# Hybrid sub-block of a two-layer net: SSD tiles of two head pairs, dt's exponentials behind the last silu, outputs split four chunks at a time

## The chip, the cores and the metric

One core of a Trainium2 chip runs the whole program. The metric is device microseconds (us) of one execution. Engines: TensorE (PE, with its weight loader PEld) multiplies, VectorE (DVE) and ScalarE (ACT) do elementwise work, GpSimd (POOL) a few masks, and SyncE (SP) issues the DMAs. Each engine runs its instructions strictly in the order in which the program lists them.

## The reference, cut to what matters

256 tokens of width 1024 pass through six sub-blocks (FFN, hybrid, FFN; FFN, mLSTM, FFN), each with a modulated RMS norm before it and a gated residual after it, all in float32. The change lies in the hybrid:

```
gate_lru, x_lru, z_ssd, xbc, dt_raw = split(h @ w_in)
y_lru = rg_lru(conv(x_lru)) * gelu(gate_lru)          # a_t, u_t = gates; h_t = a_t h_{t-1} + u_t, u has a sqrt
xbc   = silu(conv(xbc));  xs, B, C = split(xbc)       # 16 heads of 64, 2 groups, state 128
dt    = softplus(dt_raw + bias);  a = -exp(a_log)
y     = ssd_chunked(xs, dt, a, B, C) + d * xs         # 2 chunks of 128 tokens
y     = rms_norm over each group (512 wide) of y * silu(z_ssd)
out   = concat(y_lru, y) @ w_out
```

Within a chunk, ssd multiplies the scores C B^T by decays exp(-relu(acs_t - acs_s)) under the causal mask, with acs the running sum of dt*a; the state that the first chunk leaves enters the second through exp(acs).

## The kernel before, in words

Activations lie transposed, as chunks of 128 channels by 256 tokens. Each matrix product is made of three in a reduced float32 type: with `hi` the rounded value and `lo` the rest, hi*hi + hi*lo + lo*hi (`multiply`, L363 to L365). So every operand is split in two: ScalarE copies `hi`, VectorE subtracts for `lo`. Weights arrive as one stream of pieces of eight 128x128 tiles (`Weights`): SP issues the DMA (`wraw`, four buffers), ScalarE makes `whi` (L99), VectorE `wlo` (L100), six pieces ahead at most. A piece is first touched when the code asks for a tile about four pieces before it. The modulation vectors of later sub-blocks are made beside this on VectorE (`ada`, L229), where a plan of due pieces puts them.

The order of instructions on each engine is fixed when the program is built: a planner walks its own model of time and gives a free engine the ready instruction that comes first in the code. `add_manual_dep` and `issue_after` add edges to it, and `in_one_go` chains several TensorE instructions. A tile of a tag with one buffer cannot be written before every reader and writer of the tile that had the buffer is done.

The hybrid (`hybrid`, L649 on) runs as follows. The first four projections give B and C. `xbc_pair` projects two chunks of xs, then dt's projection follows (L689 to L691), its transposes (L696), and dt's small chain: an exponential of -|dt| (L634), `log1p_series` (L616 to L628, some 14 dependent VectorE instructions), dt (L708), acs by a product with a triangle (L713, L714), the decay `dec` (L720, L721), and the transposed sums `stk` (L727). Beside it run the same series for the LRU's lambda (`hc`) and, from L744, the other six chunks of xs (`project`, then `conv`: one ScalarE and three VectorE instructions, then a silu, L670).

Then comes the loop over c = 0..9 (L803): it projects `xl` and `z` of chunk c and makes the LRU gates of chunk c-2 (`lru_gates`). At c = 1 and 3 it also transposes four chunks of xs and multiplies by dt (`ssd_values`, L768), and at c = 2 and 4 makes the state (`ssd_state`, L781).

The loop over pairs m0 = 0, 2, 4, 6 (L831) makes the SSD output of two chunks, that is four heads: matmuls `ab` spread the sums over partitions (L839), ScalarE makes `mt` (four Relu and one Exp for each m, L847 and L849) and `ce` (L851), VectorE multiplies them by the scores and by C (L852, L855), TensorE adds up `y` in one bank (L866, L879), VectorE gates it (L881), ScalarE squares it (`add_square`), and `project` makes the LRU's gelu input `gl`. After two pairs, `rs_tokens` sums the squares on TensorE and computes 1/sqrt in 12 small VectorE instructions (`rsqrt_small`, L282 to L289). `group_norm` spreads the root by a matmul (`rsb_g`) and scales four chunks of xs (L827).

At last `out_project` adds four parts into eight half banks: ys 0 to 3, ys 4 to 7, then LRU outputs 0 and 1, and 2 to 7. Beside part 0, `lru(0, d)` takes the square roots (L912, L913), multiplies (L915) and scans (L917); before d = 4 it normalises and splits ys 4 to 7. Beside part 1, `lru(1, d)` applies gelu (L924), multiplies (L925) and splits into `ylb`.

Two buffers are shared: `ysb`, the split ys, takes the buffer of `ssd` (xdt, the state, B and C), and `ylb` that of `aq` (the LRU's a and roots).

Of the kernel before, what the change touches and what calls it, by code (L numbers as in the profile page):

```python
# [134 lines left out]
def body(ctx: ExitStack, tc: tile.TileContext, a, out, dbg=None):  # L135
# [223 lines left out]

    def multiply(dst, both, start, stop):  # L360

        wh, wl = W.next()
        m = nc.tensor.matmul(dst, wh, both[:, 0, :], start=start, stop=False, skip_group_check=True)  # L363
        nc.tensor.matmul(dst, wh, both[:, 1, :], start=False, stop=False, skip_group_check=True)  # L364
        nc.tensor.matmul(dst, wl, both[:, 0, :], start=False, stop=stop, skip_group_check=True)  # L365
        return m
# [282 lines left out]
    def hybrid(s, acc, sp, wk):  # L649
# [25 lines left out]

        def xbc_pair():
            two = [mm_bank(f"xbc{i}") for i in range(2)]
            project_two(two, h)
            for i, b in enumerate(two):
                xbc(xs[:, i, :], b[:, 0:T], i)  # L680

# [11 lines left out]
        nc.scalar.copy(dtt, b[:, 0:T])  # L693
        b = ax_bank("dt")
        for tb in range(2):
            nc.tensor.transpose(b[:, tb * P:(tb + 1) * P], dtt[:, tb * P:(tb + 1) * P], ident)  # L696
# [4 lines left out]
        e, e_ins = exp_neg_abs(dt, [P, 2, 16], "dt")  # L701
        with tc.issue_after(e_ins):
# [41 lines left out]
        for i in range(2, 8):  # L744
            b = mm_bank(f"xbc{i}")
            behind = project(b[:, 0:T], h)
            xbc(xs[:, i, :], b[:, 0:T], i)
# [9 lines left out]
        in_one_go(turned[4:] + turned[2:4] + turned[:2], [ready, behind])  # L757
# [5 lines left out]
        def ssd_values(g):  # L763
# [8 lines left out]
            xw = wk.tile([P, 512], F32, tag="mt", name=f"xw{g}", bufs=4)  # L772
# [30 lines left out]
        for c in range(8 + LRU_LAG):  # L803
# [27 lines left out]
        for m0 in range(0, 8, 2):  # L831
            g = m0 // 4
            pair = (m0, m0 + 1)
            decays, states, eyes, needed = [], [], [], []
# [6 lines left out]
            for m, b in zip(pair, ab):  # L841

                mt = wk.tile([P, 2, 2, P], F32, tag="mt", name=f"mt{m}", bufs=4)
                for i in range(2):
                    for c in range(2):
                        hd = 2 * m + i
                        nc.scalar.activation(mt[:, i, c, :], b[:, i * T + c * P:i * T + (c + 1) * P], AF.Relu,  # L847
                                             bias=acs[:, c, hd:hd + 1], scale=-1.0)
                nc.scalar.activation(mt, mt, AF.Exp, scale=-1.0)  # L849
                ce = wk.tile([P, 2, P], F32, tag="ce", name=f"ce{m}", bufs=2)  # L850
                expo = nc.scalar.activation(ce, b.rearrange("p (i t) -> p i t", i=2)[:, :, P:T], AF.Exp)  # L851
                needed += [nc.vector.tensor_tensor(  # L852
                    out=mt.rearrange("p i c t -> p i (c t)"), in0=mt.rearrange("p i c t -> p i (c t)"),
                    in1=cb[:, g].rearrange("p c t -> p (c t)").unsqueeze(1).to_broadcast([P, 2, T]), op=ALU.mult)]
                needed += [nc.vector.tensor_tensor(out=ce, in0=ce,  # L855
                                                   in1=bc[:, 2 + g, P:T].unsqueeze(1).to_broadcast([P, 2, P]),
                                                   op=ALU.mult)]
                dg = wk.tile([P, P], F32, tag="dg", name=f"dg{m}", bufs=2)
                with tc.issue_after(W.normed.ins):
                    nc.scalar.activation(dg, ident, AF.Copy, scale=col("ssd_d", m))  # L860
                decays.append(mt)
                states.append(ce)
                eyes.append(dg)

            bank = ax_bank(f"y{m0}", "p")
            in_one_go([nc.tensor.matmul(bank[:, n * T:(n + 1) * T], dg, xs[:, m, :], start=(n == 0), stop=False,  # L866
                                        skip_group_check=True) for n, (m, dg) in enumerate(zip(pair, eyes))], [])

            products = []
            for n, (m, mt, ce) in enumerate(zip(pair, decays, states)):  # L870
                b = bank[:, n * T:(n + 1) * T]
                for c in range(3):
                    for i in range(2):
# [3 lines left out]
                        dst, lw, v = ((b[r, 0:P], xdt[:, 0, w], mt[:, i, 0, :]), (b[r, P:T], xdt[:, 1, w], mt[:, i, 1, :]),  # L877
                                      (b[r, P:T], st[:, g, ws], ce[:, i, :]))[c]
# [13 lines left out]
            if m0 % 4 == 2:  # L892
                roots.append(rs_tokens(gacc, 512, f"g{g}", "q"))
# [3 lines left out]
        ys = [split(xs[:, m, :], ysb[:, m]) for m in range(4)]  # L897
# [4 lines left out]
        def lru(n, c):  # L902
            if n == 0:
                if c == 4:

                    group_norm(1)
                    ys.extend(split(xs[:, m, :], ysb[:, m]) for m in range(4, 8))
                if c == 0:
                    with tc.issue_after(expo.ins):
                        for q in range(2):  # L910
                            v = nq[:, 4 * q:4 * q + 4, :].rearrange("p c t -> p (c t)")
                            nc.vector.tensor_scalar(out=v, in0=v, scalar1=-1e-35, scalar2=None, op0=ALU.min)  # L912
                            sqrt = nc.scalar.activation(v, v, AF.Sqrt, scale=-1.0)  # L913
                    last.append(sqrt.ins)
                nc.vector.scalar_tensor_tensor(out=nq[:, c, :], in0=xl[:, c, :], scalar=0.5, in1=nq[:, c, :],  # L915
                                               op0=ALU.mult, op1=ALU.mult)
                nc.vector.tensor_tensor_scan(out=xl[:, c, :], data0=av[:, c, :], data1=nq[:, c, :], initial=0.0,  # L917
                                             op0=ALU.mult, op1=ALU.add)
# [441 lines left out]
```

## Time and profile before

| | us |
|---|---|
| median of 3 runs | 1113.64 (1113.23 to 1114.13) |
| profiled execution | 1112.73 |
| its span, first to last instruction | 1111.0 |
| hybrid, first B/C projection to last output projection | about 196 to 376 |
| PE busy in the span | 1093.8 (98%) |
| DVE busy | 925.8 (83%) |
| ACT busy | 659.3 (59%) |
| mean granted TensorE clock | 0.997 |

Times in the profile are microseconds from the start of the span unless marked ns. A row of a timeline gives the start, the duration, the engine, the line and operation, output and inputs, the shapes, the count of merged instructions, and in brackets the idle time before it with what ended it. A row of waits gives who waited for whom, the sum, the count and the longest. A row of groups gives the busy time and the mean ns of one, then idle time ahead. Matmuls overlap: each is shown with 276 ns while they start about 110 ns apart, so what is lost on TensorE is seen in the waits and in the number of starts.

### The profile page before, as it was taken

How to read it: one execution, taken by the hardware profiler on the slowest of the kernel's cores; microseconds unless marked ns; L12 is line 12 of the kernel's file. 1: busy time of each engine (PE TensorE's matmuls, PEld its weight loads, DVE VectorE, ACT ScalarE, POOL GpSimd, SP SyncE). 2: the span in 40 equal slices, each digit the busy share in tenths (PEclk: the TensorE clock that was granted, in tenths of full speed). 3: DMA queues.
4: the chain of work that ended last, by engine and by line, in shares of the span. 5: the costliest groups of instructions: out<-in, count | busy, mean ns of one | idle time of the engine just before them, and what ended most of it. 6: DMA issues, size and time to landing. Idle time of an engine off the chain costs nothing.

```text
span 1111.0 us, 23486 instructions
## 1 busy us (share of the span) xinstructions
PE 1093.8 (98%) x9366; PEld 1078.4 (97%) x9366; DVE 925.8 (83%) x1735; ACT 659.3 (59%) x1097; POOL 9.4 (1%) x29
## 2 busy tenths in 40 slices
PE   8999999999999999999999999999999999999997
PEld 7999999999989999999999999999999999999997
DVE  7999999899899899989789988869867978766552
ACT  5664545688995565554454544548778655455442
POOL 0000000000000000000000000010000000000000
PEclk9999999999999999999999999999999999999999
DMA  9999999556555579999759998962432464865651
GB/s 372 338 327 362 377 359 339 182 188 194 198 190 176 181 260 388 351 344 338 279 157 346 307 333 309 313 204 98 153 96 93 157 231 147 281 229 194 196 180 38
DMA packets 75279, 272.35 MB, mean 245 GB/s; under 512 B 8449, under 2 KB 9121, under 8 KB 75170
## 3 DMA queue, kind: packets, MB, share of 16 engines
q1 hardware_dynamic: 74304, 269.22, 69.3%
q8 instruction: 73, 1.20, 0.4%
q0 software_dynamic: 432, 1.10, 0.4%
q10 hardware_dynamic: 434, 0.53, 0.1%
q14 instruction: 36, 0.29, 0.1%
HBM read 269.77 MB, written 1.05 MB: 244 GB/s over the span
## 4 chain that ended last, share of the span: by engine, by line
PE 84%; ACT 7%; DVE 6%; issue 2%; DMA 1%; POOL 0%; ACTq 0%; DVEq 0%; SPq 0%; POOLq 0%
PE gu L364 13%; PE gu L365 13%; PE gu L363 12%; PE od L364 10%; PE od L363 10%; PE od L365 10%; DVE wlo L100 2%; ACT whi L99 1%; DMA wraw<-in_wst_dram 1%; PE gu_f L425 1%; PE gu_f L426 1%; PE gu_f L427 1%; PE up L363 1%; PE up L364 1%; PE up L365 1%
## 5 line engine op out<-in xcount | busy, mean ns | idle before, releaser
L100 DVE TENSOR_TENSOR wlo<-wraw,whi 128x1024 fp32r<-128x1024 f32 x366 | 445.9, 1222 | 93.5 <-ACT whi L99 91.5
L99 ACT CAST whi<-wraw 128x1024 fp32r<-128x1024 f32 x364 | 379.4, 1049 | 226.4 <-DMA wraw<-in_wst_dram 74.1
L364 PE MATMUL gu<-hb,whi 128*128 128x256 f32 x1312 | 360.9, 276 | 1.2 <-DVE hb L560 1.2
L365 PE MATMUL gu<-hb,wlo 128*128 128x256 f32 x1312 | 360.6, 276 | 0.0
L363 PE MATMUL gu<-hb,whi 128*128 128x256 f32 x1312 | 357.8, 277 | 1.1 <-ACT whi L95 0.5
L364 PEld LDWEIGHTS gu<-hb,whi 128*128 128x128 f32 x1312 | 246.3, 188 | 1.8 <-DVE hb L560 1.8
L365 PEld LDWEIGHTS gu<-hb,wlo 128*128 128x128 f32 x1312 | 246.3, 188 | 0.0
L363 PEld LDWEIGHTS gu<-hb,whi 128*128 128x128 f32 x1312 | 244.2, 188 | 2.1 <-ACT whi L95 0.7
L363 PE MATMUL od<-ph,whi 128*128 128x256 f32 x704 | 194.3, 276 | 0.0
L364 PE MATMUL od<-ph,whi 128*128 128x256 f32 x704 | 194.3, 276 | 0.0
L365 PE MATMUL od<-ph,wlo 128*128 128x256 f32 x704 | 194.3, 276 | 0.0
L229 DVE SCALAR_TENSOR_TENSOR ada<-ada,cact 128x1024 f32<-128x1024 f32 x144 | 175.3, 1219 | 0.2 <-DMA ada<-in_adaT_dram 0.2
L363 PEld LDWEIGHTS od<-ph,whi 128*128 128x128 f32 x704 | 132.2, 188 | 0.0
L364 PEld LDWEIGHTS od<-ph,whi 128*128 128x128 f32 x704 | 132.2, 188 | 0.0
L365 PEld LDWEIGHTS od<-ph,wlo 128*128 128x128 f32 x704 | 132.2, 188 | 0.0
L356 ACT CAST ph<-fg 128x256 fp32r<-128x256 f32 x88 | 35.6, 410 | 102.2 <-DVE fg L507 100.0
L357 DVE TENSOR_TENSOR ph<-fg,ph 128x256 fp32r<-128x256 f32 x88 | 36.9, 422 | 13.1 <-ACT ph L356 12.9
L483 DVE SCALAR_TENSOR_TENSOR x<-od,gate,x 128x256 f32<-128x256 f32 x48 | 23.0, 482 | 25.4 <-PE od L365 25.4
L346 ACT ACTIVATE sq_o<-x 128x256 f32<-128x256 f32 x42 | 17.6, 418 | 42.3 <-DVE x L483 40.3
L365 PE MATMUL zz<-hb,wlo 128*128 128x256 f32 x128 | 36.0, 282 | 0.0
L364 PE MATMUL zz<-hb,whi 128*128 128x256 f32 x128 | 36.0, 281 | 0.0
L363 PE MATMUL zz<-hb,whi 128*128 128x256 f32 x128 | 35.9, 281 | 0.0
(424 smaller groups left out, 1996.3 us busy)
## 6 DMA issues: line engine op xcount, KB each, us to landing
wraw<-in_wst_dram SPq DMA_DIRECT2D x366, 512.0 KB, 4.6
ada<-in_adaT_dram SPq DMA_DIRECT2D x144, 512.0 KB, 5.6
xn<-in_x_dram SPq DMA_DIRECT2D x2, 512.0 KB, 4.0
wgr<-in_ml_wg_dram POOLq DMA_DIRECT2D x3, 256.0 KB, 3.7
out_dram<-res ACTq DMA_DIRECT2D x2, 128.0 KB, 2.4
out_dram<-res SPq DMA_DIRECT2D x2, 128.0 KB, 2.1
out_dram<-res SPq DMA_DIRECT2D x1, 256.0 KB, 2.5
out_dram<-res ACTq DMA_DIRECT2D x1, 256.0 KB, 2.6
```

Of the source, the lines that this page charges most:

```text
L99: raw_hi = nc.scalar.copy(hi, raw)
L100: self.last = nc.vector.tensor_tensor(out=lo, in0=raw, in1=hi.bitcast(F32), op=ALU.subtract)
L229: return nc.vector.scalar_tensor_tensor(out=raw, in0=raw, scalar=1.0, in1=cact, op0=ALU.mult, op1=ALU.mult, accum_out=mods[s][:, m:m + 1])
L346: square = nc.scalar.activation(q, x, AF.Square).ins
L356: nc.scalar.copy(hi, src)
L357: nc.vector.tensor_tensor(out=both[:, 1, :], in0=src, in1=hi.bitcast(F32), op=ALU.subtract)
L363: m = nc.tensor.matmul(dst, wh, both[:, 0, :], start=start, stop=False, skip_group_check=True)
L364: nc.tensor.matmul(dst, wh, both[:, 1, :], start=False, stop=False, skip_group_check=True)
L365: nc.tensor.matmul(dst, wl, both[:, 0, :], start=False, stop=stop, skip_group_check=True)
L425: nc.tensor.matmul(dst, wh, rh, start=(k == 0), stop=False)
L426: nc.tensor.matmul(dst, wh, rl, start=False, stop=False)
L483: nc.vector.scalar_tensor_tensor(out=xs_t[d], in0=dst, scalar=g[:, d:d + 1], in1=xs_t[d], op0=ALU.mult, op1=ALU.add)
```

## The change

All of it is in `hybrid`.

1. The six remaining xbc projections (`xbc_rest`) come in the code directly behind the copy of dt's projection. dt's two transposes are chained behind that copy, and the exponential of -|dt| is put behind the last silu on ScalarE. `ssd_values` moves from c = 1, 3 to c = 2, 4 and `ssd_state` from c = 2, 4 to c = 3, 5.
2. `mt`, `ce` and `dg` are tiles of two m (four heads): one Exp and one product over 1024, one product over 512 for `ce`; the Relu, the exponentials of `ce` and the copies into `dg` stay single. The squares of a pair are one instruction, and the sums of squares are kept for two chunks side by side.
3. ys 0 to 3 are split by one ScalarE and one VectorE instruction (`split_wide`), and so are ys 4 to 7. The square roots of the LRU are put behind the first of these on ScalarE. The LRU's multiplication by the root takes four chunks at once, gelu, its product and the split of `ylb` two.

The arithmetic on each element is the same.

```
+    def split_wide(src, both):
+        hi = nc.scalar.copy(both[:, :, 0, :], src)
+        nc.vector.tensor_tensor(out=both[:, :, 1, :], in0=src, in1=both[:, :, 0, :].bitcast(F32), op=ALU.subtract)
+        return hi
...
+        def xbc_rest():
+            for i in range(2, 8):
+                b = mm_bank(f"xbc{i}")
+                m = project(b[:, 0:T], h)
+                behind[:] = [m, xbc(xs[:, i, :], b[:, 0:T], i)]
...
-        nc.scalar.copy(dtt, b[:, 0:T])
+        copied = nc.scalar.copy(dtt, b[:, 0:T])
+        xbc_rest()
         b = ax_bank("dt")
-        for tb in range(2):
-            nc.tensor.transpose(b[:, tb * P:(tb + 1) * P], dtt[:, tb * P:(tb + 1) * P], ident)
+        in_one_go([nc.tensor.transpose(b[:, tb * P:(tb + 1) * P], dtt[:, tb * P:(tb + 1) * P], ident)
+                   for tb in range(2)], [copied])
...
         e, e_ins = exp_neg_abs(dt, [P, 2, 16], "dt")
+        tc.add_manual_dep(e_ins, behind[1].ins.name, NOSYNC, reason="the silus first")
...
-            if c in (1, 3):
-                xw = ssd_values(c // 2)
             if c in (2, 4):
+                xw = ssd_values(c // 2 - 1)
+            if c in (3, 5):
                 ssd_state(c // 2 - 1, xw)
...
+            mt = wk.tile([P, 2, 2, 2, P], F32, tag="mt", name=f"mt{m0}", bufs=2)
+            ce = wk.tile([P, 2, 2, P], F32, tag="ce", name=f"ce{m0}", bufs=2)
+            dg = wk.tile([P, 2, P], F32, tag="dg", name=f"dg{m0}", bufs=2)
...
+            nc.scalar.activation(mt, mt, AF.Exp, scale=-1.0)
+            heads = mt.rearrange("p n i c t -> p (n i) (c t)")
+            needed = [nc.vector.tensor_tensor(
+                out=heads, in0=heads, in1=cb[:, g].rearrange("p c t -> p (c t)").unsqueeze(1).to_broadcast([P, 4, T]),
+                op=ALU.mult)]
...
-                gacc = [sp.tile([P, T], F32, name=f"gacc{g}")]
-            for m in pair:
-                add_square(gacc, xs[:, m, :], m % 4, 4, f"g{m}")
+                gacc = sp.tile([P, 2, T], F32, tag="gacc", name=f"gacc{g}")
+                nc.scalar.activation(gacc, xs[:, m0:m0 + 2, :], AF.Square)
+            else:
+                q = wk.tile([P, 2, T], F32R, tag="xlb", name=f"sq2_{g}", bufs=LRU_LAG + 1).bitcast(F32)
+                nc.scalar.activation(q, xs[:, m0:m0 + 2, :], AF.Square)
+                nc.vector.tensor_tensor(out=gacc, in0=gacc, in1=q, op=ALU.add)
...
-        ys = [split(xs[:, m, :], ysb[:, m]) for m in range(4)]
+        made = split_wide(xs[:, 0:4, :], ysb[:, 0:4])
+        ys = [ysb[:, m] for m in range(8)]
...
-                    ys.extend(split(xs[:, m, :], ysb[:, m]) for m in range(4, 8))
+                    split_wide(xs[:, 4:8, :], ysb[:, 4:8])
...
                             sqrt = nc.scalar.activation(v, v, AF.Sqrt, scale=-1.0)
+                            tc.add_manual_dep(sqrt.ins, made.ins.name, NOSYNC, reason="the first outputs first")
...
-                nc.vector.scalar_tensor_tensor(out=nq[:, c, :], in0=xl[:, c, :], scalar=0.5, in1=nq[:, c, :],
-                                               op0=ALU.mult, op1=ALU.mult)
+                if c % 4 == 0:
+                    nc.vector.scalar_tensor_tensor(out=nq[:, c:c + 4, :], in0=xl[:, c:c + 4, :], scalar=0.5,
+                                                   in1=nq[:, c:c + 4, :], op0=ALU.mult, op1=ALU.mult)
...
-                t = sz[:, c, :]
-                with tc.issue_after(last[0]):
-                    nc.scalar.activation(t, t, AF.Gelu_apprx_tanh)
-                nc.vector.tensor_tensor(out=xl[:, c, :], in0=xl[:, c, :], in1=t, op=ALU.mult)
-                yl.append(split(xl[:, c, :], last[1][:, c]))
+                if c % 2 == 0:
+                    two = slice(c, c + 2)
+                    with tc.issue_after(last[0]):
+                        nc.scalar.activation(sz[:, two, :], sz[:, two, :], AF.Gelu_apprx_tanh)
+                    nc.vector.tensor_tensor(out=xl[:, two, :], in0=xl[:, two, :], in1=sz[:, two, :], op=ALU.mult)
+                    split_wide(xl[:, two, :], last[1][:, two])
+                yl.append(last[1][:, c])
```

More of the change, by code (lines that the diff above doesn't have):

```diff
@@ L756, in hybrid @@
                                                bc[:, 2 + g, c * P:(c + 1) * P], start=True, stop=True))
-        in_one_go(turned[4:] + turned[2:4] + turned[:2], [ready, behind])
+        in_one_go(turned[4:] + turned[2:4] + turned[:2], [ready, behind[0]])
         cb = sp.tile([P, 2, 2, P], F32, name="cbt")
@@ L840, in hybrid @@
                                      start=True, stop=True)
-            for m, b in zip(pair, ab):
-                mt = wk.tile([P, 2, 2, P], F32, tag="mt", name=f"mt{m}", bufs=4)
+            mt = wk.tile([P, 2, 2, 2, P], F32, tag="mt", name=f"mt{m0}", bufs=2)
+            ce = wk.tile([P, 2, 2, P], F32, tag="ce", name=f"ce{m0}", bufs=2)
+            dg = wk.tile([P, 2, P], F32, tag="dg", name=f"dg{m0}", bufs=2)
+            for n, (m, b) in enumerate(zip(pair, ab)):
                 for i in range(2):
@@ L852, in hybrid @@
[L852 to L857, printed above, removed]
@@ L865, in hybrid @@
             bank = ax_bank(f"y{m0}", "p")
[L866 to L867 removed]
+            in_one_go([nc.tensor.matmul(bank[:, n * T:(n + 1) * T], dg[:, n, :], xs[:, m, :], start=(n == 0),
+                                        stop=False, skip_group_check=True) for n, m in enumerate(pair)], [])
             products = []
[L870 removed]
+            for n, m in enumerate(pair):
```

31 lines of the change are left out of this document (13 added, 18 removed).

## The prediction

> **What bounds the kernel now.** I read the page first, then what the weight loader waits for inside the hybrid stage (209 to 362 us of the span), then busy times by stretch, then the order of instructions on ScalarE, TensorE and VectorE around each wait. The page's busy times and its chain of waits:
>
> ```profile
> PE 1093.8 (98%) x9366; PEld 1078.4 (97%) x9366; DVE 925.8 (83%) x1735; ACT 659.3 (59%) x1097; POOL 9.4 (1%) x29
> PE 84%; ACT 7%; DVE 6%; issue 2%; DMA 1%; POOL 0%; ACTq 0%; DVEq 0%; SPq 0%; POOLq 0%
> ```
>
> TensorE sets the time, so only TensorE idle time and clock can be won. The change touches the hybrid stage alone. The loader's waits there, 209 to 362 us (total us, times, longest):
>
> ```profile
> PEld od L363 <- ACT ysb L356: 1.9, 1, 1.9
> PEld ri L363 <- ACT xlb L356: 0.9, 1, 0.9
> PEld dt L696 <- ACT dtt L693: 0.8, 1, 0.8
> PEld od L363 <- ACT ssd_z L891: 0.6, 1, 0.6
> PEld ri L364 <- DVE xlb L357: 0.5, 1, 0.5
> ...
> PEld ab L839 <- ACT ce L851: 0.4, 1, 0.4
> ```
>
> These six sum to 5.1 us. Everything else that the change saves on ScalarE or VectorE is behind a TensorE that is busy. Two ordinary stretches (us, then busy time of PE, PEld, DVE, ACT, POOL with counts, PEclk, DMA share, GB/s):
>
> ```profile
> 236.00:250.00 14.00, 14.00 (x126) 14.00 (x125) 13.25 (x27) 10.73 (x18) 0.00 (x0) 1.00 0.60 202
> ...
> 274.00:289.00 15.00, 15.00 (x134) 15.00 (x134) 14.80 (x26) 13.22 (x25) 0.00 (x0) 1.00 0.71 240
> ```
>
> TensorE is full, and VectorE nearly so: it is the second bound, and work that is only shifted on it does not disappear. Then the clock, in stretches of 3.4 us:
>
> ```profile
> 322.00:325.40 3.40, 3.40 (x31) 3.28 (x29) 3.40 (x9) 3.37 (x9) 0.00 (x0) 1.00 0.79 300
> 326.80:330.20 3.40, 1.41 (x11) 0.97 (x7) 3.21 (x6) 3.40 (x10) 0.00 (x0) 1.00 0.47 154
> 332.00:335.40 3.40, 3.40 (x19) 3.40 (x17) 3.40 (x11) 1.54 (x3) 0.00 (x0) 0.50 0.06 18
> ```
>
> After the wait for ysb the granted clock is 0.50 for 3.4 us, and 19 matmuls start in place of 31: 12/31 of 3.4 us, **1.3 us** lost on top of the 2.5 us of the two od waits. This corner, 326 to 336 us, holds 3.8 of the 6.4 us to be had.
>
> **The change part by part.** *dt behind the last silu.* The two transposes (L696) move behind 144 matmuls of xbc, so their wait of 0.8 us goes. On ScalarE the Exp, Silu, Exp, Silu, Exp order becomes one Exp. Table loads before:
>
> ```profile
> L634 ACT ACT_TABLE_LOAD x1 | 1.3, 1283 | 0.0
> L721 ACT ACT_TABLE_LOAD x1 | 1.3, 1283 | 0.0
> L796 ACT ACT_TABLE_LOAD x1 | 1.3, 1283 | 0.0
> ```
>
> With the two at L670 that is five, of which four go: 5.1 us of ScalarE, hidden behind a full TensorE, so worth nothing by themselves; they shorten a few VectorE waits for ScalarE. SP's queue keeps its order: the six moved projections carry their weight pieces and ada blocks with them, and the dt steps issue no DMA. What is late next is dt itself. Its chain and its first use, on ScalarE and VectorE:
>
> ```profile
> 226.66 0.23 ACT L634 ACTIVATE ena_dt<-ena_dt 128x32 f32<-128x32 f32 x1
> ...
> 245.52 0.41 ACT L670 ACTIVATE ssd_x<-ssd_x 128x256 f32<-128x256 f32 x1
> ```
>
> ```profile
> 235.20 0.18 DVE L708 SCALAR_TENSOR_TENSOR dt<-l1s_dt,dt 128x32 f32<-128x32 f32 x1
> ...
> 251.42 0.69 DVE L768 TENSOR_TENSOR ssd<-xn,dt 128x512 f32<-128x512 f32 x1
> ```
>
> From the exponential to dt took 8.5 us. Behind a last silu at 245.5 and one load, the exponential ends near 247.3 at the latest, dt is there by 255.9. The first use moves one LRU round later (54 matmuls at 3.4/31 us, 5.9 us): 257.3. Cover 1.4 us; if it is gone, TensorE waits in its transposes or in the acs matmuls behind one VectorE instruction, 1.2 us (the long ones below).
>
> *Upstream in all*: the dt, ri and ab waits sum to 2.6 us. Bounds: all of it won (-2.6), or nothing won and one such new wait (+1.2). A full VectorE would turn the 0.8 us of dt into a longer wait of ri for xlb; against that stand 0.75 us of VectorE idle time in the first stretch alone. I take **-0.9**, dt's wait and little of the others.
>
> *Tiles of two pairs.* Per pair of m, two mt exponentials, two mt products, two ce products and two squares each become one of double width. On VectorE four steps of 0.33 us become one of 1.14 (both from rows below): 0.07 us per merged instruction, some 0.3 us a pair; the eight Relu and two ce stay. One wide product must wait for the wide exponential, so y's inputs come no sooner. TensorE fills these stretches with gl projections. Zero, within -0.4 (ab's wait, already counted above) and +0.6 (half of a 1.2 us wide instruction no longer overlapped).
>
> *First outputs ahead of the roots.* ScalarE and TensorE at that place:
>
> ```profile
> 323.96 1.28 ACT L913 ACT_TABLE_LOAD   x1
> 325.25 2.00 ACT L913 ACTIVATE lru_aq<-lru_aq 128x1024 f32<-128x1024 f32 x2
> 327.17 1.03 ACT L99 CAST whi<-wraw 128x1024 fp32r<-128x1024 f32 x1
> 328.10 0.40 ACT L356 CAST ysb<-ssd_x 128x256 fp32r<-128x256 f32 x1
> ```
>
> ```profile
> 326.55 0.39 PE L879 MATMUL y<-ce,ssd 128*64 128x128 f32 x4
> 328.55 0.51 PE L363 MATMUL od<-ysb,whi 128*128 128x256 f32 x2 [1.62 <-ACT ysb L356]
> ```
>
> ysb has the tag of ssd with one buffer, so no split can write it before the last y product has read ssd, 326.94. ScalarE is then free (gl copies come earlier): one copy of 1024, 1.03 us, ends at 328.0; first od at 328.0 in place of 328.55, and four chunks are ready at once, so the 0.6 us behind it goes too: -1.15. The low half follows on VectorE after another 1.2 us, while 16 products with the high half take 1.8 us; if the order on TensorE does not put those first, up to 1.2 us is lost. Bounds -1.15 to 0.1; I take **-0.9**. *Clock*: 0 or **-1.3**; I take the latter.
>
> *The second half of ys* is what is late next. How the 142 od matmuls with ysb from 338.38 run, and VectorE before them:
>
> ```profile
> 338.38:354.90 16.52, 16.38 (x142) 1.00 0.58 183
> ```
>
> ```profile
> L917 DVE TENSOR_TENSOR_SCAN lru_x<-lru_aq 128x256 f32<-128x256 f32 x3 | 2.0, 681 | 0.0
> L915 DVE SCALAR_TENSOR_TENSOR lru_aq<-lru_x,lru_aq 128x256 f32<-128x256 f32 x4 | 1.6, 415 | 0.0
> L357 DVE TENSOR_TENSOR ysb<-ssd_x,ysb 128x256 fp32r<-128x256 f32 x3 | 1.2, 418 | 0.0
> L100 DVE TENSOR_TENSOR wlo<-wraw,whi 128x1024 fp32r<-128x1024 f32 x1 | 1.2, 1216 | 0.0
> ```
>
> ```profile
> 338.80 1.65 DVE L827 SCALAR_TENSOR_TENSOR ssd_x<-ssd_x,cols,rsb_g 128x256 f32<-128x256 f32 x4
> 340.37 1.42 DVE L357 TENSOR_TENSOR ysb<-ssd_x,ysb 128x256 fp32r<-128x256 f32 x4
> ```
>
> 192 od matmuls read ysb, 96 a half; 46 of the 142 belong to the first, so the second begins at 338.38 + 46 x 16.52/142 = 343.7. After the change TensorE is there 0.9 + 1.3 sooner, 341.5. Ready, with the norm at its old place: 338.80 + 1.65 + a copy of 1.05 = 341.5. Before, chunk by chunk, low halves began at 340.37; a wide split gives that overlap away. So the slack is spent exactly, and the norm's place decides. Its root is a chain of 12 small VectorE instructions (331.0 to 337.1), and the 11 rows counted above, 331.04 to 337.02, lie one between each two links. Four splits in 1.42 us make a step of 0.33 us, 0.08 under the length of one; so a scan is a step of 0.6 and a 1024-wide row one of 1.14. Seven of the eleven (nq and ysb) are steps of 0.33 that the change merges away. If seven scans take their gaps, the chain grows by 7 x 0.27 = 1.9; if two wide nq, two more wlo and three scans do, by 4 x 1.14 + 3 x 0.6 - 7 x 0.33 = 4.0. If instead the roots, now later on ScalarE, leave the gaps empty, a link costs 0.20, as here in the next stage:
>
> ```profile
> 379.55 0.17 DVE L284 TENSOR_SCALAR rsy_n<-rsw_n 128x2 int32<-128x2 int32 x1
> 379.75 0.16 DVE L287 TENSOR_TENSOR rsw_n<-rsy_n 128x2 f32<-128x2 f32 x1
> ```
>
> That is 2.4 us in place of 6.1, -3.7. I take **+0.5**, just above the middle, so a new wait of 0.5 us; bounds 0 and 4.0, 5.2 if the low half counts as well. Behind it VectorE has 20 instructions fewer (nq, ysb, the gelu products, ylb), 0.07 us each, 1.4 us: over half of TensorE's lead at ylb.
>
> **Sum**: -0.9 - 0.9 - 1.3 + 0.5 = -2.6. The profiled execution took 1112.73 us (span 1111.0 and 1.7 around it), so 1110.1; the median of the runs is 0.9 above that execution, so **1111.0 us**.
>
> On the clock the Trainium skill says (TensorE: Matmul & The Clock Gate, Part 1: The HAM clock gate) that half rate comes after at least one idle window of about 3.4 us and ends after about 3.4 us of work. The second half agrees with the 3.4 us at 0.50 above; the first does not, since TensorE did 11 matmuls in the stretch before. Taken literally, it would let the clock fall in the first rival below and not in the forecast, and would leave the sum at -2.6.
>
> **The rivals.** *1. The wait moves to the second half of ys (slower).* Place: od at ys 4 to 7, for the copy behind the second norm. For it: no 0.33 us steps are left as fill. Against it: the roots come 2 us later. With +4.0, the wait is 4.0 us, longer than the one that halved the clock, so 1.3 more; with -0.5 upstream: -0.5 - 0.9 - 1.3 + 4.0 + 1.3 = +2.6, **1116.2**. With the forecast's 0.9 upstream the sign turns once the wait passes 1.8 us and the clock falls (1.8 + 1.3 = 0.9 + 0.9 + 1.3).
> *2. The early split does not do what it says.* It still waits for y, 1.6 us of idle time remain, and the clock falls all the same. For it: the tag. Against it: 2.5 us become 1.6. Then TensorE reaches the second half at 342.8, no wait there: -1.8, **1111.8**, not to be told from none.
> *3. dt too late.* The cover of 1.4 us is gone, VectorE stays the bound upstream: +1.2 - 0.9 - 1.3 + 0.5 = -0.5, **1113.1**.
>
> **How the numbers follow.** This kernel's measurement tells 0.2%, 2.2 us, from no change. Forecast 0.44 (its own range 1109.0 to 1112.2; 0.35 of it faster, 0.09 same), rival 1 0.24 (0.18 slower, 0.06 same, since its wait can be anything up to 4.0), rival 2 0.18 (0.05 faster, 0.13 same), rival 3 0.14 (0.10 same, 0.04 slower). Faster 0.40, same 0.38, slower 0.22. Low end: -2.6 upstream with -1.15 and -1.3 is -5.0, 1108.6; high end, rival 1's price, 1116.2. Range 1108.5 to 1116.2.
>
> **What would show it.** dt's wait absent and one Exp load near 243 to 247; first od within 1.5 us of the last y; no stretch at clock 0.50 by 336; a wait of od for ysb near 341, under 1 us. Wrong if that wait is over 1.8 us, if the clock falls to 0.50 anywhere from 326 to 350, or if acs or the xn transposes wait for VectorE.

## The result, and the profile after

The changed kernel takes **1122.32 us** (median of 4 runs, 1121.41 to 1123.61), the kernel before 1113.82 beside it (1113.23 to 1114.13): ratio **1.0076, 95% interval 1.0063 to 1.0088**, 8.5 us slower. The profiled execution took 1122.86 us, with a span of 1121.1.

The engines' totals on the page of the changed kernel:

```profile
PE 1097.7 (98%) x9366; PEld 1081.8 (96%) x9366; DVE 924.0 (82%) x1705; ACT 653.3 (58%) x1071; POOL 9.3 (1%) x29
```

The change did what it says: 30 VectorE and 26 ScalarE instructions fewer, TensorE's count the same. It is TensorE that stood still for longer. What the loader waits for between 209 and 375 us (total us, times, longest):

```profile
PEld od L369 <- ACT ysb L362: 4.7, 2, 3.3
PEld rsb_g L337 <- issue: 2.1, 1, 2.1
PEld od L370 <- DVE ysb L363: 1.9, 2, 1.0
PEld y L892 <- DVE mt L869: 0.9, 1, 0.9
PEld acs L731 <- DVE l1s_dt L728: 0.9, 1, 0.9
PEld ri L369 <- ACT xlb L356: 0.6, 1, 0.6
```

dt's wait is gone, those for acs and for the spread of the second root (rsb_g) are new, and y's has grown from 0.3 us. These rows sum to 11.1 us; the six of before summed to 5.1. Windows of the same trace (us, busy time by engine, then the granted clock):

```profile
332.00:335.40 3.40, 3.40 (x20) 3.40 (x19) 2.43 (x3) 2.29 (x5) 0.00 (x0) 0.54 0.26 100
348.00:352.00 4.00, 1.22 (x4) 0.93 (x4) 4.00 (x8) 1.48 (x2) 0.00 (x0) 0.67 0.54 163
352.00:356.00 4.00, 3.59 (x17) 3.59 (x18) 3.99 (x8) 1.25 (x2) 0.00 (x0) 0.50 0.54 169
```

The old fall of the clock after the first wait is still there, and a second one follows. Over both, two-microsecond windows of the trace add up to 5.1 us of lost clock, where before had 1.7. So the ledger reads: waits 6.0 us more, clock 3.4 us more, 9.4 in all. It is rough: in the second stretch at half clock, 6.83 us from 349.33, TensorE was busy for 4.97 us only, so up to 0.9 us is counted twice. The milestones put 9.65 us, all of the difference, in the hybrid. All times count from the first B/C matmul (at 195.99 us before, 196.44 after):

| us after the first B/C matmul | before | after | later by |
|---|---|---|---|
| last y product starts | 130.67 | 132.11 | 1.4 |
| second root's chain starts on VectorE | 135.00 | 140.17 | 5.2 |
| root spread by a matmul (rsb_g, the last of four) | 142.38 | 150.28 | 7.9 |
| second group norm starts | 142.80 | 151.38 | 8.6 |
| od matmuls of ys 4 to 7 start | 147.75 | 154.17 | 6.4 |
| last od matmul with ysb | 158.51 | 168.17 | 9.7 |
| next sub-block's first projection | 180.39 | 190.04 | 9.65 |

After that projection both profiles take 734.6 us. How the lateness arises, on ScalarE (start, duration):

```profile
328.87 1.04 ACT L362 CAST ysb<-ssd_x 128x1024 fp32r<-128x1024 f32 x1 [1.34 <-PE y L892]
329.93 1.28 ACT L930 ACT_TABLE_LOAD   x1
331.23 1.06 ACT L930 ACTIVATE lru_aq<-lru_aq 128x1024 f32<-128x1024 f32 x1
332.19 0.61 ACT L901 ACTIVATE sq<-ssd_x 128x512 f32<-128x512 f32 x1
...
349.51 1.05 ACT L362 CAST ysb<-ssd_x 128x1024 fp32r<-128x1024 f32 x1 [1.07 <-DVE ssd_x L841]
```

The squares of the last pair, from which the second root is made, now stand behind the wide copy, a table load and a root: they start at 332.19. Before, they started 0.3 us after the first copy of one chunk (328.10):

```profile
328.40 0.72 ACT L346 ACTIVATE sq_g<-ssd_x 128x256 f32<-128x256 f32 x2
```

On TensorE, after:

```profile
335.57 1.00 PE L314 MATMUL rst_g<-ones,gacc 128*128 128x1 f32 x8
...
346.32 0.68 PE L337 MATMUL rsb_g<-ident,rsy_g 128*128 128x128 f32 x4 [1.89 <-DVE rsy_g L289]
...
350.61 0.80 PE L369 MATMUL od<-ysb,whi 128*128 128x256 f32 x2 [3.14 <-ACT ysb L362]
```

The sum of squares comes late behind 25 od matmuls, 15 of them at half clock (before, it stood behind 4); VectorE had its input ready at 334.14, so it stood ready in the queue for 1.4 us. The spread holds up the last od matmuls of the first half: 92 of the 96 stand ahead of it, 50 before. Then the second half has nothing to work on. Between the two stands VectorE:

```profile
336.61 0.16 DVE L326 TENSOR_SCALAR rsv_g<-rst_g 128x2 f32<-128x2 f32 x1 [1.86 <-PE rst_g L314]
...
338.64 1.22 DVE L934 SCALAR_TENSOR_TENSOR lru_aq<-lru_x,lru_aq 128x1024 f32<-128x1024 f32 x1
...
346.04 0.13 DVE L289 SCALAR_TENSOR_TENSOR rsy_g<-rsw_g,rsy_g 128x2 f32<-128x2 f32 x1
346.09 0.68 DVE L945 TENSOR_TENSOR lru_x<-lru_x,ssd_z 128x512 f32<-128x512 f32 x1
346.69 1.22 DVE L100 TENSOR_TENSOR wlo<-wraw,whi 128x1024 fp32r<-128x1024 f32 x1
347.82 1.65 DVE L841 SCALAR_TENSOR_TENSOR ssd_x<-ssd_x,cols,rsb_g 128x256 f32<-128x256 f32 x4
```

The first and the last link of before:

```profile
330.99 0.16 DVE L326 TENSOR_SCALAR rsv_g<-rst_g 128x2 f32<-128x2 f32 x1 [0.87 <-PE rst_g L314]
...
337.03 0.13 DVE L289 SCALAR_TENSOR_TENSOR rsy_g<-rsw_g,rsy_g 128x2 f32<-128x2 f32 x1
```

From the start of the first of the twelve links to that of the last, 9.4 us pass, 6.0 before. In both kernels every gap holds a longer instruction, and two more stand ahead of the norm. After, the eleven gaps hold seven scans and four instructions of 1.2 us; before, they held seven steps of 0.4 us, three scans and one of 1.2. The low half of the wide split starts only at 351.14, so its wait follows the 3.3 us for the high half.

### The profile page after: what moved, and what is told of

Read it like the earlier page. It is cut to its first block, busy times and chain, and to the rows that moved or that the text cites. A ratio compares the mean times of both kernels' runs of the same rounds, so it can differ in the third digit from the quotient of the medians.

```text
span 1121.1 us, 23441 instructions
## 1 busy us (share of the span) xinstructions
PE 1097.7 (98%) x9366; PEld 1081.8 (96%) x9366; DVE 924.0 (82%) x1705; ACT 653.3 (58%) x1071; POOL 9.3 (1%) x29
## 4 chain that ended last, share of the span: by engine, by line
PE 85%; DVE 8%; ACT 4%; issue 2%; DMA 1%; ACTq 0%; SPq 0%; DVEq 0%
PE gu L370 13%; PE gu L371 12%; PE gu L369 12%; PE od L370 10%; PE od L371 9%; PE od L369 9%; DVE wlo L100 3%; PE gu_f L431 1%; PE gu_f L432 1%; PE gu_f L433 1%; PE up L370 1%; PE up L369 1%; DVE ada L229 1%; PE up L371 1%; ACT whi L99 1%
```

## The experiments

In the diffs, an edge marked NOSYNC only orders two instructions of one engine. Medians stand beside a kernel before of 1114.49 in the first group, of 1113.61 for `no_tiles`, `bare`, `free` and `splits_bare`, of 1113.79 for the four with "low" or "late" in the name, of 1113.77 for the last four. Theory A in the first expectations: the third part carries most, since it starts the root's chain late, fills its gaps with long steps and leaves TensorE waiting at the second half.

### The parts one by one

`only_dt`, `only_tiles` and `only_splits` are the kernel before with part 1, 2 or 3 of the change; `no_splits` has parts 1 and 2, `no_tiles` parts 1 and 3.

```
 only_dt:      + xbc_rest() ahead of dt's transposes, the edge behind the last silu, ssd_values at c = 2, 4
 only_tiles:   + mt, ce, dg and the squares of two m at a time
 only_splits:  + split_wide for ys and ylb, the roots behind the first copy, four root products at a time
```

> The kernel before with part 1 alone (xbc_rest ahead of dt's transposes, dt's exponential behind the last silu, values and state one round later). Theory A, the split part carries the loss: dt's wait of 0.8 us goes and one of about 0.9 us for acs comes, so within 2 us of the kernel before (1112 to 1116). Theory B, the loss comes from dt being late and VectorE's load moving downstream: 2.5 us or more slower (above 1116.3). Theory C, the parts only hurt together: within 2 us.

> The kernel before with part 2 alone (mt, ce, dg and the squares two chunks wide). Theory A: the wide mt product keeps the last y waiting about 0.9 us, the rest is unchanged, so 0 to 2 us slower (1114 to 1116). Theory B, y being late is what starts the loss: 3 us or more slower (above 1117). Theory C: within 2 us.

> The kernel before with part 3 alone (ys split four wide, square roots behind the first split, root products four wide, gelu and ylb two wide). Theory A: the second norm starts late, behind the roots, and its chain is filled with long steps; od waits for the second half of ys and the clock falls: 5 to 9 us slower (1119 to 1123). Theory B: at most 3 us slower. Theory C: at most 3 us slower.

> The changed kernel without part 3 (parts 1 and 2 together). Theory A: -1 to +3 us against the kernel before (1113 to 1117). Theory B: 5 us or more slower (above 1119). Theory C, only the three together hurt: within 2 us.

> The changed kernel without part 2 (parts 1 and 3 together). If the parts add up: 0.07% and 0.28%, 1118.3. If parts 1 and 3 hurt each other (one more long step in the chain, a longer wait over which the clock falls a second time): 1120 or more. If it is part 2 that makes part 3 worse: 1118.5 or less.

| kernel | median us | ratio and interval | norm starts | second half starts | next sub-block |
|---|---|---|---|---|---|
| before | | | 142.80 | 147.75 | 180.39 |
| only_dt | 1115.34 | 1.0007, 0.9998 to 1.0016 | 144.73 | 149.76 | 182.40 |
| only_tiles | 1115.61 | 1.0014, 1.0004 to 1.0023 | 146.68 | 149.27 | 181.91 |
| only_splits | 1117.59 | 1.0028, 1.0017 to 1.0039 | 146.48 | 149.76 | 184.49 |
| no_splits | 1117.43 | 1.0025, 1.0014 to 1.0035 | 148.34 | 151.20 | 183.84 |
| no_tiles | 1118.34 | 1.0040, 1.0025 to 1.0055 | 147.33 | 150.56 | 185.32 |
| after | 1122.32 | 1.0076, 1.0063 to 1.0088 | 151.38 | 154.17 | 190.04 |

No part gains. The third alone costs most, 3.1 us, but not the 5 to 9 that theory A expected. The three add up to 0.49% where the whole costs 0.76: behind the first two parts the third costs about 0.5%, alone 0.28%. Parts 1 and 3 together (`no_tiles`) cost 0.40%, about their sum of 0.35; so the surplus appears when the tiles come to the rest, 0.36% in place of 0.14 alone. These differences lie at the edge of what the intervals tell. `only_dt`, `only_tiles` and `no_splits` came out as theory A expected, the last at its upper edge. The waits of `only_splits` from 320 us on, and of `only_dt` the one new row:

```profile
PEld od L369 <- ACT ysb L362: 3.6, 2, 2.2
PEld od L370 <- DVE ysb L363: 1.6, 2, 1.1
PEld rsb_g L337 <- issue: 1.4, 1, 1.4
```

```profile
PEld acs L725 <- DVE l1s_dt L722: 1.4, 1, 1.4
```

The first three are the pattern of the changed kernel, smaller. The last is what became of dt's 0.8 us: TensorE meets the missing dt in the acs matmuls.

### What stands in the chain's gaps, and what stands behind it

`bare` (on the changed kernel) and `splits_bare` (on `only_splits`) put the root products behind the last link. `after_low`, `splits_low` and `roots_low` put products and scans behind the low half of ys 4 to 7; the last is the kernel before with one-chunk splits and the roots held back. `free` is the changed kernel without the edge that holds back the roots, `roots_late` the kernel before with nothing but that edge.

```
 bare, splits_bare, at the root product m:
+    tc.add_manual_dep(m.ins, rsqrt_ends[-1].ins.name, NOSYNC, reason="the root first")
 after_low, splits_low, roots_low:
+    tc.add_manual_dep(m.ins, low_half_of_ys_4_to_7.ins.name, NOSYNC, reason="the norm first")
 free:
-    tc.add_manual_dep(sqrt.ins, made.ins.name, NOSYNC, reason="the first outputs first")
 roots_late, roots_low (made: the fourth copy of one chunk):
+    tc.add_manual_dep(sqrt.ins, made.ins.name, NOSYNC, reason="the first outputs first")
```

> The changed kernel with the LRU's root products (and so its scans) put behind the end of the second norm's root chain on VectorE; the program then lists ten of the chain's twelve steps without anything between. Theory A, the wait of od for the second half of ys is the chain's start plus what fills its gaps: the chain from its first step to the spread matmul falls from 10.1 us to 4 to 6, od's second half begins 4 us sooner, the second fall of the clock shrinks or goes: 5 to 8 us faster than the changed kernel (1115 to 1118). Theory B, the start of the chain (behind roots and squares) is what counts, not its fill: under 2 us faster (above 1120.5).

> The changed kernel without the edge that puts the square roots behind the first split. Theory A: the roots run while ScalarE is idle before the last y ends, the squares of the last pair come sooner, the chain starts 2 to 4 us sooner, but its gaps stay filled with long steps: 2 to 4 us faster than the changed kernel (1118.5 to 1120.5). Theory B, the chain's start is all: 5 us or more faster (under 1117.5).

> The kernel before with part 3 alone and the same edge (root products behind the root chain); all twelve steps of the chain stand together. Theory A: the second half of ys is ready before TensorE asks, only the first wait of about 1.4 and 1.1 us and its fall of the clock stay: 0 to 3 us faster than the kernel before, 3 to 6 us faster than part 3 alone. Theory B: as part 3 alone, 3 us slower than the kernel before.

> The changed kernel with one thing put elsewhere: the two wide root products and the eight scans that follow them stand on VectorE behind the low half of ys 4-7 instead of in the gaps of the second group norm's chain. Theory A (what fills and follows that chain on VectorE makes the two late waits of the od matmuls): the chain takes about 2.4 us as it does where nothing fills it, the norm and the low half follow directly, the waits for rsb_g and for the second half of ys fall under 0.5 us each, the second fall of the clock at 348 to 356 goes, and about 5 us come back: 1117 to 1118, about what the first two parts cost without the third (1117.43). Rival B (the loss sits ahead of the chain, in the first od wait and the late squares, and what is behind it only passes it on): 1119.6 to 1121, and a wait for the second half of ys stays over 1.5 us.

> The kernel before with the third part alone, and the root products and scans behind the low half of ys 4-7. Theory A: of the 4 us that the third part costs alone, both late waits go (rsb_g 1.4, low half 1.6 to 2.4) and the clock's second fall with them; the earlier first outputs then pay at last: the first od wait stays near 1.4+1.2 us with no half clock behind it: 1111.5 to 1113, at or below the kernel before. Rival B (wide splits and late roots cost by themselves, whatever follows): 1115 to 1117.

> The kernel before with the splits of one chunk kept, the roots held behind the fourth of the first outputs' copies, and the root products and scans behind the low half of ys 4-7. Theory A: as the wide splits without their later second half: the first od wait is that of before (1.9+0.6) or less, no wait for the second half: 1111.5 to 1113. Rival B (the chain's late start carries the cost): 1114.5 to 1116.

> The kernel before with one edge of the third part alone: the roots of the LRU are held behind the copies of the first four outputs; splits of one chunk, products and scans as before. Theory A: the edge alone moves the second norm's chain by 1 to 2 us (the squares stand behind the table load and the root), the filled chain passes that on to the norm, and half of it reaches the od matmuls: 1114 to 1115.5. Rival B (the edge is free, the wide splits carry the third part's 4 us): 1113.2 to 1114. Rival C (the edge carries nearly all of it): over 1116.5.

| kernel | median us | ratio and interval | chain starts | chain to spread | norm starts | second half starts | next sub-block |
|---|---|---|---|---|---|---|---|
| before | | | 135.00 | 7.38 | 142.80 | 147.75 | 180.39 |
| after | 1122.32 | 1.0076, 1.0063 to 1.0088 | 140.17 | 10.11 | 151.38 | 154.17 | 190.04 |
| bare | 1119.57 | 1.0050, 1.0035 to 1.0065 | 140.03 | 5.85 | 146.19 | 151.31 | 187.37 |
| free | 1118.72 | 1.0043, 1.0026 to 1.0060 | 138.14 | 9.58 | 148.22 | 151.48 | 185.22 |
| after_low | 1118.83 | 1.0042, 1.0026 to 1.0057 | 139.64 | 4.96 | 145.32 | 149.26 | 182.66 |
| splits_bare | 1116.21 | 1.0021, 1.0012 to 1.0031 | 136.33 | 4.16 | 143.20 | 146.10 | 182.83 |
| splits_low | 1117.69 | 1.0028, 1.0017 to 1.0038 | 137.84 | 4.16 | 142.31 | 147.57 | 181.26 |
| roots_low | 1116.18 | 1.0016, 1.0008 to 1.0025 | 136.85 | 3.10 | 141.42 | 145.53 | 182.41 |
| roots_late | 1114.27 | 1.0002, 0.9993 to 1.0011 | 136.90 | 8.02 | 145.55 | 147.33 | 180.12 |

The chain can be as short as the forecast's lower bound. Rows of `splits_low`, first and last link and the norm:

```profile
334.78 0.16 DVE L326 TENSOR_SCALAR rsv_g<-rst_g 128x2 f32<-128x2 f32 x1 [2.39 <-PE rst_g L314]
...
336.95 0.16 DVE L289 SCALAR_TENSOR_TENSOR rsy_g<-rsw_g,rsy_g 128x2 f32<-128x2 f32 x1
...
339.25 1.66 DVE L833 SCALAR_TENSOR_TENSOR ssd_x<-ssd_x,cols,rsb_g 128x256 f32<-128x256 f32 x4 [0.96 <-PE rsb_g L337]
```

2.2 us in place of 6.0, and both late waits of od for ysb are gone. Yet this kernel is as slow as `only_splits`: my expectation of 1111.5 to 1113 failed, and that for `roots_low` with it. Where the time went, in its waits, its windows and the first residual step of the next norm (the profiled execution is the slowest of the ten, 1119.72 us, so these sizes are those of a bad case; the quickest took 1115.05):

```profile
PEld rst_n L314 <- ACT sq_o L346: 2.5, 1, 2.5
...
PEld od L370 <- DVE ylb L363: 0.5, 1, 0.5
```

```profile
330.00:340.00 10.00, 9.31 (x67) 9.31 (x68) 6.08 (x18) 8.52 (x13) 0.00 (x0) 0.83 0.46 141
380.00:388.00 8.00, 6.27 (x29) 6.27 (x30) 4.57 (x18) 1.05 (x3) 0.00 (x0) 0.61 0.24 80
```

```profile
367.85 0.48 DVE L489 SCALAR_TENSOR_TENSOR x<-od,gate,x 128x256 f32<-128x256 f32 x1
```

The same of the kernel before, a window and the same step:

```profile
330.00:340.00 10.00, 9.99 (x72) 9.79 (x72) 9.13 (x30) 7.79 (x16) 0.00 (x0) 0.83 0.34 111
```

```profile
363.22 0.48 DVE L483 SCALAR_TENSOR_TENSOR x<-od,gate,x 128x256 f32<-128x256 f32 x1
```

With its gaps empty, VectorE works 6.08 of 10 us where it worked 9.13. Those 3 us of products, scans and weight pieces are done later on an engine that is full from 340 to 360 us in both, so the residual steps begin 4.6 us later (3.7 counted from the first B/C matmul), the next norm's sum waits 2.5 us in place of 0.4, and the clock falls there, at 380 to 388. `after_low`, whose profile is again its slowest execution, shows the same row with 3.7 us, `roots_low` has 3.1 us for ylb and 1.1 for that sum. The milestones of the table miss this loss: behind the next sub-block's first projection `splits_low` and `after_low` take 5 to 6 us more than the kernel before. So the fill of the kernel before was not wasted: it kept VectorE at work. `splits_bare` leaves the products and scans directly behind the short chain; there they hold the norm back instead (143.20, before 142.80), and od waits 2.4 us for the low half of the wide split.

Theory A has a part of it wrong, then. On part 3 alone, *emptying* the gaps gave nothing clear of noise. On the changed kernel it gave 2.8 us (`bare`, 5 to 8 expected) and 3.5 us (`after_low`, about 5 expected), a part of the loss only. Whether the empty gaps or the lateness of the moved work costs more, these runs do not tell apart. The edge that holds the roots back costs nothing that can be told from noise by itself (`roots_late`: the chain starts 1.9 us later, but the two first od waits shrink and lie apart, and the clock does not fall). In the changed kernel, taking the edge away gave back about 3.6 us (`free`, as expected); the same edge thus has no price of its own.

### How wide the steps are

`after_chunk` is the changed kernel with ys 4 to 7 split one chunk at a time. `after_chunk_nq` has the root products one chunk at a time as well. `splits_chunk_nq` has of the change only the third part, with both taken back. `tiles_thin` has only the second part, its wide buffers kept, but mt's exponential and the products for one m at a time.

```
 after_chunk, after_chunk_nq, splits_chunk_nq:
-    split_wide(xs[:, 4:8, :], ysb[:, 4:8])
+    for m in range(4, 8):
+        split(xs[:, m, :], ysb[:, m])
 after_chunk_nq, splits_chunk_nq:
-    if c % 4 == 0:
-        nc.vector.scalar_tensor_tensor(out=nq[:, c:c + 4, :], in0=xl[:, c:c + 4, :], ...)
+    nc.vector.scalar_tensor_tensor(out=nq[:, c, :], in0=xl[:, c, :], ...)
 tiles_thin, inside the loop over m:
+    nc.scalar.activation(mt[:, n], mt[:, n], AF.Exp, scale=-1.0)      # and both products, for one n
```

> The changed kernel, but the outputs 4 to 7 are split one chunk at a time, as before. Theory C (the width of the second half's split makes its wait: a copy of 1.05 us that needs all four norms, then a subtraction of 1.22 us): the first high half comes about 1.9 us sooner, the first low half about 2.5 us sooner, so the two waits of 3.4 and 1.4 us shrink to about 1.5 and 0.4, and if the idle stays small the clock's fall at 348 to 356 (3 us) goes too: 1116.5 to 1120. Rival (the chain is so late that any split of the second half waits): 1121 to 1122.5 with the wait over 2.5 us.

> As the last, and the root products one chunk at a time (about 0.48 us in a gap of the chain instead of 1.22). Theory C: the chain takes 1 to 2 us less than the 9.4 us of the changed kernel, the norm comes as much sooner, and what is left is the late chain's start: 1115.5 to 1119, below the run before it by 0 to 1.5. Rival (the filler's length does not matter, since VectorE's work is only moved): equal to the run before it within 0.7.

> The kernel before with of the third part only the late roots, the wide split of outputs 0 to 3 and the steps of two chunks on the LRU's outputs; the second half's splits and the root products as before. Theory C: the third part's 4 us are the width of the second half and of the products, so this is 1113.5 to 1115. Rival (the wide first split, by holding back VectorE and ScalarE ahead of the squares, carries it): 1116.5 to 1118.

> The kernel before with the tiles' part alone, its buffers for two head pairs kept, but the exponential and the products with CB and C done for one head pair at a time. If y's wait for the wide product (0.9 us, and 0.96 us of y's end) is what that part costs: the wait falls to about 0.3, 1113.5 to 1114.5. Rival (the squares of two chunks and the other moves of the part carry it): 1115 to 1116.

| kernel | median us | ratio and interval | chain starts | chain to spread | norm starts | second half starts | next sub-block |
|---|---|---|---|---|---|---|---|
| after | 1122.32 | 1.0076, 1.0063 to 1.0088 | 140.17 | 10.11 | 151.38 | 154.17 | 190.04 |
| after_chunk | 1119.96 | 1.0050, 1.0035 to 1.0065 | 140.24 | 10.12 | 151.46 | 152.43 | 187.10 |
| after_chunk_nq | 1116.17 | 1.0017, 1.0008 to 1.0027 | 139.87 | 7.78 | 149.31 | 150.29 | 183.67 |
| splits_chunk_nq | 1114.44 | 1.0003, 0.9993 to 1.0012 | 136.48 | 8.03 | 145.92 | 147.71 | 180.81 |
| tiles_thin | 1114.95 | 1.0012, 1.0002 to 1.0023 | 132.67 | 7.53 | 140.84 | 144.99 | 179.68 |

This shows what cost in the third part. Taking back two merges, of 4 splits and of 8 products, returns 6.1 us of the changed kernel's 8.5: 2.4 for the splits (the second half starts 1.7 us sooner with the norm where it was, and the second fall of the clock lasts 3.4 us in place of 6.8), 3.8 for the products (chain 2.3 us shorter, norm 2.2 sooner, no second fall of the clock). The products gave more than the 1.5 us at most that was expected of them, and the clock's part came with them. In `after_chunk_nq` the gaps hold five products of 0.4 us, four scans and two instructions of 1.2 us. `after_chunk` and `splits_chunk_nq` came within what was expected. What is left, 1.0017, is about what parts 1 and 2 cost by themselves, 1.0025; and without those two the rest of the third part is free, 1.0003. Waits of `after_chunk_nq`, and its norm and split on VectorE:

```profile
PEld od L369 <- ACT ysb L362: 1.4, 1, 1.4
PEld acs L731 <- DVE l1s_dt L728: 1.3, 1, 1.3
PEld rsb_g L337 <- issue: 1.3, 1, 1.3
PEld od L370 <- DVE ysb L363: 1.0, 1, 1.0
PEld y L892 <- DVE mt L869: 0.9, 1, 0.9
...
PEld od L370 <- DVE ysb L357: 0.5, 1, 0.5
```

```profile
345.68 1.65 DVE L841 SCALAR_TENSOR_TENSOR ssd_x<-ssd_x,cols,rsb_g 128x256 f32<-128x256 f32 x4
347.25 0.76 DVE L357 TENSOR_TENSOR ysb<-ssd_x,ysb 128x256 fp32r<-128x256 f32 x2
```

The 3.3 us for the second high half is gone, and the first low halves follow the norm at once. VectorE loses no time by it: 19.76 of 20 us busy from 336 to 356.

`tiles_thin` settles nothing. Its ten runs lie between 1113.06 and 1118.79, its profile is of the quickest of them, and its interval covers that of `only_tiles` (1.0014). y's wait for the wide product is no longer among its waits, but whether this is what the tiles cost stays open.

## Why the prediction was wrong

The forecast was 1111.0 us, faster; the changed kernel took 1122.3, 6.1 us above the range. Step by step:

**The norm "at its old place".** This is the step that failed. The prediction took 338.80 as the norm's start and moved TensorE alone. The norm started at 347.82, 8.6 us later counted from the first B/C matmul: 5.2 because the chain started later, 2.7 because it took longer up to the spread, 0.7 because the weight piece ahead of the norm ended 1.1 us after the spread's last matmul began, 0.4 before. The 5.2 had no term at all: 1.4 of it came with the later y, 1.9 with the copy, load and root ahead of the squares, 0.6 with their sum on VectorE behind a wide product, 1.3 with the place of rst_g in TensorE's queue. The prediction even counted the roots' delay in its favour ("the roots come 2 us later"), and did not ask what else stands behind the wide copy, table load and root on ScalarE: the squares that feed the very chain. Nor did it see that rst_g and rsb_g stand in TensorE's own queue, one behind 25 od matmuls, the other in front of the last four of the first half, where TensorE waited 2.1 us.

**+0.5 for the fill.** Bounds 0 and 4.0; measured 9.4 in place of 6.0 us, +3.4 from first to last link, and `after_chunk_nq` shows that shorter fill, not empty gaps, gives most of it back. "Just above the middle" was a choice with no row for it; the row count with two wide nq and more wlo, which gave 4.0, was near. Its 5.2 "if the low half counts as well" was short too: rsb_g, high half and low half together made 2.1 + 3.3 + 1.0 = 6.4 us.

**-1.3 for the clock.** The gain did not come: 17 matmuls start from 332.00 to 335.40 where 16 did (the counts of the windows, 20 and 19, take in those already under way, so the prediction's 12 lost of 31 were too few: 3.41 us at 0.50 are worth 1.7 us, not 1.3). The loss came twice, 3.4 us more than before.

**-0.9 for the first od wait.** The split does begin right behind y, as forecast, and 1.9 us became 1.4. But only two matmuls with the high half ran before one needed the low half, not 16, so the old second wait of 0.6 became 1.0: "if the order on TensorE does not put those first" was the case. Gain 0.1 us.

**-0.9 upstream.** Right that dt's wait goes and that one Exp load remains before the loop (at 240.26); part 1, which saves the table loads, gains nothing by itself. Wrong on the cover: 1.4 us was worked out for the first use in ssd_values, but the acs matmuls come sooner. TensorE reached them at 250.4 and waited till 251.28. The last y product is 1.4 us later, not 0.9 sooner. That part 1 costs 0.07% by itself is not told from nothing; that parts 1 and 2 together cost 0.25% is.

**Zero for the tiles.** y waits 0.9 us for the wide product, beyond the +0.6 that was the bound; alone the part costs 0.14%.

**Rival 1** had the mechanism, the place and the second fall of the clock; its 1116.2 lacked the chain's start (5.2) and the wait at the spread. Rival 2's outcome, a clock that falls all the same, came with it. Rival 3's came as the wait of acs. All three marks named as "wrong if" showed up in the trace. The weighing went wrong because each mishap was priced alone: late y, late squares, a long chain and a late split lie on one path, and the whole costs more (0.76%) than `no_splits` and `only_splits` add up to (0.53%), at the edge of the intervals.

On the clock the prediction set the Trainium skill's rule (TensorE: Matmul & The Clock Gate, Part 1: The HAM clock gate: a whole idle window of about 3.4 us) beside its own. Here the measurement decides against the literal rule, since the clock fell to 0.50 at 332.26 after waits of 1.4 and 1.0 us with two matmuls between them. The same section says that the window runs free of the program, so that a transition depends on where in the window the work lands; that agrees with what the last section shows.

## What to carry to other kernels

When the engine that feeds the bound is itself full, merging small instructions saves little (here 1.8 us of VectorE's 925.8): ask instead which short instructions were the fill of a dependent chain, and what length takes their place in each gap. Here fill mostly of 0.4 to 0.7 us did best, more fill of 1.2 us delayed the chain, and empty gaps, with the work put off, delayed what came after. Before an instruction is moved ahead on an in-order queue, list everything behind it until the next critical chain begins; a wide split gives away the overlap by which a consumer could start with the first quarter.

## What the runs showed of the hardware

**A short wait is dear or free by its place in time.** Much the same two waits before the od matmuls had three different prices. Windows of `only_dt` (1.8 and 0.6 us of wait) and of `only_splits` (1.4 and 1.1):

```profile
330.00:337.00 7.00, 6.62 (x31) 6.33 (x31) 5.30 (x19) 4.77 (x11) 0.00 (x0) 0.57 0.28 93
```

```profile
326.00:336.00 10.00, 7.89 (x75) 7.15 (x74) 9.73 (x18) 8.91 (x13) 0.00 (x0) 1.00 0.54 170
```

About 6.8 us near half clock in the first, none in the second; the kernel before had 3.4. The half clock came in stretches of 3.41 or 6.83 us, so a wait of 2.5 us cost 0, 1.7 or 3.4 us on top of itself. The traces show what decides. Where a trace has more than one stretch at half clock, they start whole multiples of 3.41 us apart (in the changed kernel 332.26 and 349.33, 5 x 3.41). On that grid of 3.41 us, these are the windows that hold the two waits, in `only_dt` and in `only_splits`:

```profile
327.54:330.95 3.41, 1.43 (x16) 0.90 (x12) 3.18 (x8) 3.41 (x9) 0.00 (x0) 1.00 0.46 154
```

```profile
326.83:330.24 3.41, 1.90 (x26) 1.45 (x25) 3.41 (x5) 2.86 (x3) 0.00 (x0) 1.00 0.38 133
330.24:333.65 3.41, 2.81 (x22) 2.64 (x23) 3.15 (x4) 3.40 (x7) 0.00 (x0) 1.00 0.77 197
```

In `only_dt` TensorE is busy for 42% of one window, and the clock is at half in the next. In `only_splits` the edge of a window cuts the second wait, TensorE is busy for 56% and 82%, and the clock stays. From 20 to 1100 us the eighteen traces hold 19 falls: 17 come right behind a window with 26 to 50% of busy time, the other two (`before` and `only_tiles`) one window later, behind 53 and 51%. Every window at full clock with 50% or less was followed by a fall; with more, no fall came but these two. This is read off the traces (where the ends of matmuls are modelled); no run moved the wait alone. Whether the half clock then lasts one window (12 times) or two (7 times) stays open. The place differs between executions of one kernel, and so does the time: `after_low` took 1116.39 us at a mean clock of 0.999 and 1121.86 at 0.994.

**A link costs less between other work.** Alone, a link of the chain takes 0.20 us from start to start (334.78 to 336.95 over eleven, in `splits_low`). Between longer instructions it adds 0.05 to 0.07: in the changed kernel one that starts at 346.04 is followed by the next row at 346.09.
